# Lagged inputs loaded by lag for a whole slice, squares summed a tile later, remainders issued with the next cast, and other DMA charges in the planner

## The chip, the cores and the metric

The kernel runs on one core of one Trainium2 chip. The metric is device time in microseconds (us): the median of several executions of the whole program, one launch. The profile shows one further execution, which has a time of its own.

## The reference

One inference step of two trunk layers for 256 prompt frames and 32 sample frames (T = 288 columns together), width D = 2048, everything in float32. Layer 0 is attention (eight "fox" heads with forget gates, eight differential heads), layer 1 a diagonal complex state-space layer (S5) with a gated unit behind it. Each layer is adaLN (shift, scale and gate from a conditioning vector) around an RMS norm, and a residual. Cut to what the change touches:

```python
def _rmsnorm(x, g):                        # squares summed over the 2048 channels
    y = x32 * lax.rsqrt(jnp.mean(x32 * x32, axis=-1, keepdims=True) + EPS)
...
def _ssm_layer(x, c, l, isd, s_re, s_im, p):
    h, gate = _adaln(x, c, ...)
    u, z = jnp.split(h @ p['w_in_ssm'][isd], 2, axis=-1)
    y, state = _s5_sequence(u32.reshape(B, T, N_GROUPS, GROUP_CH), ...)
    y = y.reshape(B, T, D_SSM) + p['ssm_d'][isd] * u32
    g = jax.nn.gelu(y)
    glu = g * jax.nn.sigmoid(g @ p['w_glu'][isd] + p['b_glu'][isd])
    out = (glu * jax.nn.silu(z)) @ p['w_out_ssm'][isd]
    x = x + gate * out
```

`_s5_sequence` runs x[t] = a x[t-1] + B u[t], y[t] = C x[t] for 128 groups of 16 channels with 64 complex states each.

## The kernel before, in words

**Layout.** Activations lie transposed: 16 tiles of 128 channels (partitions) by 288 frames. In layer 1 the frames are reordered in blocks of LC = 8: column s * 36 + j is frame 8 j + s, so that NJ = 36 blocks stand side by side for each position s within a block.

**Main matmuls in two parts.** A weight tile `w` is [128, 4, 512], 1 MB. Each of its four quarters is cast by ScalarE to a rounded `hi` (`act.copy`), and VectorE (DVE) subtracts to get the remainder `lo` (`split_step`, L406). Activations are split likewise (`ah`, `al`). For every 128 by 128 block TensorE issues three matmuls (L473 to L475): hi by ah, hi by al, lo by ah. Eight quarters may be live (NQ), four weight buffers exist (NST), with more in the first stage. With the fourth quarter, `st_done` frees the weight buffer and `pump` issues the next weight load on SP.

**Order.** `run_jobs` (L450) goes through a list of jobs, one for each weight tile, and after every second block it calls `split_step` (casts ahead) and `side.step`, which gives a turn to side tasks: Python generators that emit a few instructions and yield until they are due. When a task is due is decided by a planner (`Plan`, `Engine.cost`): each emitted instruction adds an estimated duration to the planned time of its engine, and a task goes on when the planned time of TensorE has reached the planned end of what it waits for. The planner runs while the program is built, so its figures set only the order of instructions on each engine's queue; each engine then executes its queue in order, and semaphores make it wait where data are not there. A DMA's planned cost is bytes / 360 GB/s on one common DMA clock, with 0.6 us ahead and 2.0 us behind (L122 to L131).

**The S5 layer (from L1433).** Jobs: 16 weight tiles of w_in_ssm give u (`u_evac`), 16 give z (`z1_evac`), then 16 of w_glu and 16 of w_out_ssm. Beside them run these side tasks:
- `state_in` (L1587): for each quarter of U (four tiles) it stores U to DRAM (`ud`), loads it regrouped as `ug` with 8 DMAs of 72 KB in 144-byte pieces (in the profile MX<-ud), multiplies (xin_ps) and fills X.
- `scan` (L1627): 32 steps of small DVE instructions for each quarter.
- `slices` (L1669): for each of 16 slices matmuls y_ps from the scanned states (Xm), then stores to `yd` (8 DMAs for four slices).
- `lags` (L1567) and `inside` (L1704): the part of y from within a block of 8 frames. For each slice, TensorE multiplies blocks `kb` by inputs shifted by 0 to 3 block positions (lags): partition 32 l + c of a load holds channel c at lag l. The four groups g of 32 channels (pairs of the reference's groups) of a slice each have a load of their own, `UL[4 i + g]`, [128, 288]:

```python
sp.dma_start(UL[n], bass.AP(ud.tensor, ud.offset + row * (PAD + T),
                            [[NJ, 4], [PAD + T, 32], [1, T]]))
```

Each step and count pair of the source pattern is an axis, slowest first: 4 lags, 32 channels, 288 columns. Five such buffers lie in a freed weight buffer; three more lie in `W1r` once `state_in` is through with it (L1625). The profile names these loads UL<-ud and W1r<-ud. SP issues the loads in order with all weight loads, and a load into a used buffer waits for the matmuls that read it.
- `gelus`, `gelu` (L1726): read `yd`, add, GELU, and an `act_split` makes the GLU's ah and al. U lies in MX, so the profile calls it MX.

**Squares.** `op_evac` (L1345, end of layer 0) and `fin_evac` (L1779, end of layer 1) evacuate an output tile into the residual; then ScalarE squares it into a scratch tile (`yx` in the profile), and DVE adds the square to `ssq1` at once (for tile 0 a copy; the last tile's square goes to the sum over channels by itself, through `ssl`).

All engine calls go through one wrapper, so every instruction of the profile has line L114; tiles tell them apart.

Of the kernel before, what the change touches and what calls it, by code (L numbers as in the profile page):

```python
# [93 lines left out]
class Engine:  # L94
# [5 lines left out]
    def __getattr__(self, fn):  # L100
# [14 lines left out]
        return call  # L115

    def cost(self, fn, out, ins, outs, k):
        p = self.plan
# [3 lines left out]
        if fn == "dma_start":  # L122
            t = max([p.when(p.written, a) for a in ins] + [p.at[self.name], p.base.get(out.tensor.name, 0.0)])
            p.at[self.name] = t + (0.45 if self.name != "pool" else 1.0)
            size = n * out.shape[0] * 4 / 360e3
            if self.name == "act":
                end = t + 2.6 + 2 * size
            else:
                p.at["dma"] = max(p.at["dma"], t + 0.6) + size
                end = p.at["dma"] + 2.0  # L130
            p.note(p.written, out, end)  # L131
            for a in ins:
                p.note(p.read, a, end)
            p.last = max(p.last, end)
            return
# [118 lines left out]
def build(tc, I, O):  # L254
# [8 lines left out]
    with ExitStack() as ctx:  # L263
# [142 lines left out]
        def split_step(t, force=False):  # L406
# [12 lines left out]
            act.copy(hi, st[:, i, :])  # L419
            TT(lo, st[:, i, :], hi.bitcast(F32), ALU.subtract)  # L420
            qs.append((hi, lo))
            split["live"] += 1
            if i == 3:
                st_done(k)
                pump()
            return True

        def order_of(j):
# [21 lines left out]
        def run_jobs(upto, n_side):  # L450
            while pos["run"] < upto:
# [5 lines left out]
                if j["kind"] == "main":  # L457
# [6 lines left out]
                    for i, (n, q, k, begin, end) in enumerate(order_of(j)):  # L464
                        while len(qs) <= q:
                            if not qs:
                                side.upto(plan.when(plan.written, st_of[t]))
                            split_step(t, True)
                        if first and begin:
                            g["ps"][n] = pm.tile([128, 512], F32, tag="m", name="m")  # L470
# [7 lines left out]
                        if last and end:  # L478
                            plan.last = 0.0
                            g["evac"](n, ps[:, 0:N], c)  # L480
                        if i % 2:
                            split_step(t)
                            side.step(n_side)
# [861 lines left out]
        def op_evac(gi):  # L1345
            def ev(n, ps, c):
# [9 lines left out]
                if c == 3:  # L1356
                    sq = scratch(k % 2)[:, 0:T]
                    act.activation(sq, MX[:, slot(k), :], AF.Square)
                    if k == 0:
                        dve.tensor_copy(ssq1, sq)  # L1360
                    elif k < KT - 1:
                        TT(ssq1, ssq1, sq, ALU.add)
                    else:
                        ssl.append(sq)
                    if n == 3:
                        ready.add(("x1", gi))
            return ev

        ssl = []
        op0 = len(jobs)  # L1370
# [191 lines left out]

        def ul_bufs(t, n):

            ul_free.extend(t[:, k * T:k * T + T] for k in range(n))

        def lags():  # L1567

            zero = SZ[:, 0:6, :].rearrange("p a t -> p (a t)")
            pool.memset(zero, 0.0)  # L1570
            sp.dma_start(ud[:, :, 0:PAD].rearrange("n p t -> p n t"), zero.rearrange("p (n t) -> p n t", n=KT))
            while taken[0] is None:
                yield "w any"
            t = wst.tile([128, 2048], F32, tag="w%d" % taken[0], name="UL")
            ul_bufs(t, 5)
            for n in range(4 * KT):
                while ("ur", n // 16) not in ready or not ul_free:
                    yield "w any"
                UL[n] = ul_free.pop(0)
                row = 128 * (n // 4) + 32 * (n % 4)  # L1580
                sp.dma_start(UL[n], bass.AP(ud.tensor, ud.offset + row * (PAD + T),
                                            [[NJ, 4], [PAD + T, 32], [1, T]]))
                if n % 4 == 3:
                    ready.add(("ul", n // 4))
                yield "next any"

        def state_in():  # L1587
# [36 lines left out]
            yield  # L1624
            ul_bufs(w1r[0][0], 3)  # L1625

# [77 lines left out]
        def inside():  # L1704
# [3 lines left out]
            for i in range(KT):  # L1708
                yield from wait(("ul", i))
                kb = kbs.pop(i)  # L1710
                plan.last = max([plan.when(plan.written, UL[4 * i + g]) for g in range(4)] + [plan.when(plan.written, kb)])
                yield "dve"
                yield from room()
                tps = take([128, T], "t_ps")
                for a in range(2):
                    for g in range(4):
                        mm(tps[32 * g:32 * g + 32, 4 * a * NJ:T], kb[:, g, a], UL[4 * i + g][:, 0:T - 4 * a * NJ],
                           start=a == 0, stop=a == 1)
                ul_free.extend(UL.pop(4 * i + g) for g in range(4))
                kb_load(i + 3)  # L1720
# [58 lines left out]
        def fin_evac(gi):  # L1779
            def ev(n, ps, c):  # L1780
# [3 lines left out]
                for b, (j0, j1) in enumerate(((0, JP), (JP, NJ))):  # L1784
                    dve.scalar_tensor_tensor(xk[:, :, j0:j1], ps.rearrange("p (s j) -> p s j", s=LC)[:, :, j0:j1],
                                             gate[:, 1, k, b:b + 1], xk[:, :, j0:j1], op0=ALU.mult, op1=ALU.add)
                sq = scratch(k % 2)[:, 0:T]
                act.activation(sq, MX[:, k, :], AF.Square)
                if k == 0:
                    dve.tensor_copy(ssq1, sq)  # L1790
                elif k < KT - 1:
                    TT(ssq1, ssq1, sq, ALU.add)
                else:
                    ssl.append(sq)
            return ev
# [192 lines left out]
```

## Time and profile before

| | us |
|---|---|
| three runs | 1415.28, 1416.33, 1420.74 (median 1416.33) |
| the profiled execution | 1416.64 |
| its span | 1414.8 |
| TensorE (PE) busy | 1270.3, 90% of the span |
| VectorE (DVE) busy | 928.9, 66% |
| ScalarE (ACT) busy | 594.3, 42% |

The DMA engines moved 344.91 MB, 244 GB/s on average. PE is matmuls, PEld the weight loads of TensorE beside them, SPq the queue of DMA issues on SyncE. In a row of the stage view stand the stretch, its length, then for PE, PEld, DVE, ACT and POOL the busy time with the number of instructions, then the granted TensorE clock (1.00 is full), the mean busy share of the 16 DMA engines and GB/s. In a row of the group view stand what is written from what, the count, busy time and mean duration (ns), and behind the bar the idle time of the engine ahead of them and whose work ended it. In the view of waits stand who waited for whom, the total, how often and the longest. Shares of DMA can exceed 1 where packets overlap.

### The profile page before, as it was taken

How to read it: one execution, taken by the hardware profiler on the slowest of the kernel's cores; microseconds unless marked ns; L12 is line 12 of the kernel's file. 1: busy time of each engine (PE TensorE's matmuls, PEld its weight loads, DVE VectorE, ACT ScalarE, POOL GpSimd, SP SyncE). 2: the span in 40 equal slices, each digit the busy share in tenths (PEclk: the TensorE clock that was granted, in tenths of full speed). 3: DMA queues.
4: the chain of work that ended last, by engine and by line, in shares of the span. 5: the costliest groups of instructions: out<-in, count | busy, mean ns of one | idle time of the engine just before them, and what ended most of it. 6: DMA issues, size and time to landing. Idle time of an engine off the chain costs nothing.

```text
span 1414.8 us, 28189 instructions
## 1 busy us (share of the span) xinstructions
PE 1270.3 (90%) x11098; PEld 1112.1 (79%) x11098; DVE 928.9 (66%) x2212; ACT 594.3 (42%) x1394; POOL 32.6 (2%) x21
## 2 busy tenths in 40 slices
PE   4999899999998999998996978849979877999996
PEld 2788798887887888886896958838869847989995
DVE  4479988697786777887667618527735835455554
ACT  4434233333454454554535624413444534344341
POOL 0005000000000000000000000000000000000000
PEclk9999999999999999999998999978988978999998
DMA  9988696698889898987755877883587645877641
GB/s 316 339 304 309 211 329 249 227 336 293 313 289 312 287 317 298 337 296 271 272 178 137 287 200 174 226 205 104 181 188 201 197 150 155 293 258 266 230 148 68
DMA packets 251011, 344.91 MB, mean 244 GB/s; under 512 B 51424, under 2 KB 141552, under 8 KB 250880
## 3 DMA queue, kind: packets, MB, share of 16 engines
q1 hardware_dynamic: 238208, 313.47, 68.5%
q10 hardware_dynamic: 12672, 29.65, 5.9%
q8 instruction: 88, 1.44, 0.4%
q14 instruction: 43, 0.35, 0.1%
HBM read 307.13 MB, written 35.95 MB: 242 GB/s over the span
## 4 chain that ended last, share of the span: by engine, by line
issue 46%; PE 24%; DVE 13%; DMA 10%; ACT 4%; SPq 1%; ACTq 0%; POOL 0%; POOLq 0%; DVEq 0%
PE m L114 19%; DMA w<-in_w_in_att 5%; DVE lo L114 4%; PE mod_ps L114 3%; DVE v L114 2%; ACT hi L114 2%; DVE MX L114 2%; DMA w<-in_w_mod 2%; DVE tmpv L114 1%; DMA w<-in_w_out_att 1%; SPq L114 1%; DVE qkv L114 1%; DVE dtmp L114 1%; DMA v_d<-v 1%; DMA c_gT<-in_gT 0%
## 5 line engine op out<-in xcount | busy, mean ns | idle before, releaser
L114 PE MATMUL m<-ah,hi 128*128 128x288 f32 (+1 forms) x2304 | 717.2, 311 | 28.3 <-ACT ah L114 14.6
L114 PE MATMUL m<-ah,lo 128*128 128x288 f32 (+1 forms) x2304 | 691.8, 300 | 6.7 <-DVE lo L114 6.6
L114 PE MATMUL m<-al,hi 128*128 128x288 f32 (+1 forms) x2304 | 692.6, 301 | 0.4 <-DVE al L114 0.4
L114 DVE TENSOR_TENSOR lo<-w,hi 128x512 fp32r<-128x512 f32 x560 | 374.2, 686 | 246.3 <-ACT hi L114 236.0
L114 PEld LDWEIGHTS m<-ah,hi 128*128 128x128 f32 x2304 | 444.3, 193 | 94.9 <-issue 41.8
L114 ACT CAST hi<-w 128x512 fp32r<-128x512 f32 x560 | 326.5, 618 | 362.5 <-PE m L114 204.0
L114 PEld LDWEIGHTS m<-ah,lo 128*128 128x128 f32 x2304 | 444.9, 193 | 9.3 <-DVE lo L114 9.3
L114 PEld LDWEIGHTS m<-al,hi 128*128 128x128 f32 x2304 | 445.2, 193 | 1.6 <-DVE al L114 1.4
L114 PE MATMUL mod_ps<-w,cs 128*32 128x512 f32 x736 | 96.2, 617 | 1.9 <-DMA w<-in_w_mod 1.9
L114 DVE SCALAR_TENSOR_TENSOR qkv<-m,qkv 128x288 f32<-128x288 f32 x168 | 73.0, 452 | 26.4 <-PE m L114 26.1
L114 DVE TENSOR_TENSOR X<-X,t 128x32 f32<-128x32 f32 (+1 forms) x256 | 58.3, 228 | 8.2
L114 PE MATMUL t_ps<-UL,kb 128*32 128x288 f32 (+1 forms) x220 | 31.9, 431 | 26.1 <-DMA UL<-ud 26.1
L114 ACT ACTIVATE yx<-MX 128x288 f32<-128x288 f32 (+1 forms) x40 | 19.7, 492 | 70.0 <-DVE MX L114 70.0
L114 DVE TENSOR_TENSOR v<-pt,raw 128x512 f32<-128x512 f32 (+1 forms) x64 | 46.0, 718 | 2.5 <-DMA v_d<-v 2.2
L114 DVE SCALAR_TENSOR_TENSOR MX<-MX,c_dT,t_ps 128x288 f32<-128x288 f32 x16 | 8.2, 514 | 59.0 <-PE t_ps L114 59.0
L114 DVE TENSOR_TENSOR tmpv<-pt,raw 128x512 f32<-128x512 f32 (+1 forms) x64 | 45.9, 717 | 0.0
L114 PE MATMUL y_ps<-Xm,v 128*128 128x74 f32 x256 | 37.4, 309 | 9.1 <-ACT Xm L114 9.1
L114 PEld LDWEIGHTS y_ps<-Xm,v 128*128 128x128 f32 x256 | 35.9, 223 | 10.8 <-ACT Xm L114 10.3
L114 PEld LDWEIGHTS t_ps<-UL,kb 128*32 128x32 f32 x220 | 9.5, 124 | 43.6 <-DMA UL<-ud 35.2
L114 DVE SCALAR_TENSOR_TENSOR MX<-m,gate,MX 128x256 f32<-128x256 f32 x96 | 30.7, 362 | 18.7 <-PE m L114 18.6
L114 PEld LDWEIGHTS mod_ps<-w,cs 128*32 128x32 f32 x736 | 16.9, 110 | 29.4 <-issue 25.6
L114 DVE TENSOR_TENSOR v<-v,tmpv 128x512 f32<-128x512 f32 (+1 forms) x48 | 34.3, 714 | 1.7
(228 smaller groups left out, 921.1 us busy)
## 6 DMA issues: line engine op xcount, KB each, us to landing
w<-in_w_mod SPq DMA_DIRECT2D x128, 512.0 KB
w<-in_w_in_att SPq DMA_DIRECT2D x40, 1024.0 KB
w<-in_w_in_ssm SPq DMA_DIRECT2D x32, 1024.0 KB
w<-in_w_mod SPq DMA_DIRECT2D x28, 1024.0 KB
w<-in_w_in_att SPq DMA_DIRECT2D x48, 512.0 KB
w<-in_w_out_att SPq DMA_DIRECT2D x16, 1024.0 KB
w<-in_w_glu SPq DMA_DIRECT2D x15, 1024.0 KB
w<-in_w_out_ssm SPq DMA_DIRECT2D x13, 1024.0 KB
```

What stands on the lines that cost most here:

```text
L114: return f(*a, **k)
```

## The change

Five edits:
1. The planner charges a DMA by its pieces (contiguous runs on both sides): 12 ns and 0.142 ns an element for each, over 16 engines; and 0.6 us more ahead of it (SP, POOL and ACT queues).
2. A remainder `lo` is no longer emitted with its cast. It is kept in `rests` and emitted with the next cast, when its quarter is needed, or when the planner takes the cast to be over (`rest_due`). Freeing the weight buffer goes with the fourth remainder.
3. A square joins the sum when the next tile's square comes up (`squares`); tile 0's square is written to `ssq1` directly.
4. Lagged inputs: a buffer now holds a whole slice, [128, 4 x 288], and each of its four loads brings one lag, 32 partitions by four groups by 288. Two such buffers exist from the start, the freed weight buffer and a new tile UL1; those in W1r are gone.
5. `inside` reads `UL[i][:, g]` and gives a buffer back by slice.

```diff
+    def pieces(out, src):
+        total, run = 1, []
+        for d in out.shape:
+            total *= d
+        for a in (out, src):
+            r = 1
+            for st, n in reversed(list(a.ap)[1:]):
+                if st != r and n > 1:
+                    break
+                r *= n
+            run.append(r)
+        r = min(run)
+        return total / r * (12 + 0.142 * r) / 16e3
...
-            size = n * out.shape[0] * 4 / 360e3
+            size = self.pieces(out, ins[0])
             if self.name == "act":
-                end = t + 2.6 + 2 * size
+                end = t + 3.2 + 2 * size
             else:
-                p.at["dma"] = max(p.at["dma"], t + 0.6) + size
+                p.at["dma"] = max(p.at["dma"], t + 1.2) + size
                 end = p.at["dma"] + 2.0
...
             act.copy(hi, st[:, i, :])
-            TT(lo, st[:, i, :], hi.bitcast(F32), ALU.subtract)
             qs.append((hi, lo))
             split["live"] += 1
-            if i == 3:
-                st_done(k)
-                pump()
+            rest_step(0)
+            rests.append((k, i, st, hi, lo))
             return True
+        rests = []
+        def rest_step(left):
+            while len(rests) > left:
+                k, i, st, hi, lo = rests.pop(0)
+                TT(lo, st[:, i, :], hi.bitcast(F32), ALU.subtract)
+                if i == 3:
+                    st_done(k)
+                    pump()
+        def rest_due():
+            if rests and plan.when(plan.written, rests[0][3]) <= max(plan.at["dve"], plan.at["pe"]):
+                rest_step(len(rests) - 1)
...
                             split_step(t, True)
+                        if rests and rests[0][:2] <= (t, q):
+                            rest_step(0)
...
                         if i % 2:
+                            rest_due()
                             split_step(t)
                             side.step(n_side)
...
-                    sq = scratch(k % 2)[:, 0:T]
-                    act.activation(sq, MX[:, slot(k), :], AF.Square)
-                    if k == 0:
-                        dve.tensor_copy(ssq1, sq)
-                    elif k < KT - 1:
-                        TT(ssq1, ssq1, sq, ALU.add)
-                    else:
-                        ssl.append(sq)
+                    squares(k, MX[:, slot(k), :])
...
+        def squares(k, x):
+            for sq in sqs:
+                TT(ssq1, ssq1, sq, ALU.add)
+            sqs.clear()
+            sq = scratch(k % 2)[:, 0:T] if k else ssq1
+            act.activation(sq, x, AF.Square)
+            if k == KT - 1:
+                ssl.append(sq)
+            elif k:
+                sqs.append(sq)
...
-            ul_bufs(t, 5)
-            for n in range(4 * KT):
-                while ("ur", n // 16) not in ready or not ul_free:
+            ul_free.extend((t[:, 0:4 * T], sl.tile([128, 4 * T], F32, name="UL1")))
+            row = PAD + T
+            for n in range(KT):
+                while ("ur", n // 4) not in ready or not ul_free:
                     yield "w any"
-                UL[n] = ul_free.pop(0)
-                row = 128 * (n // 4) + 32 * (n % 4)
-                sp.dma_start(UL[n], bass.AP(ud.tensor, ud.offset + row * (PAD + T),
-                                            [[NJ, 4], [PAD + T, 32], [1, T]]))
-                if n % 4 == 3:
-                    ready.add(("ul", n // 4))
+                UL[n] = ul_free.pop(0).rearrange("p (g t) -> p g t", g=4)
+                for l in range(4):
+                    sp.dma_start(UL[n][32 * l:32 * l + 32], bass.AP(ud.tensor, ud.offset + 128 * n * row + l * NJ,
+                                                                    [[row, 32], [32 * row, 4], [1, T]]))
+                ready.add(("ul", n))
                 yield "next any"
...
-            ul_bufs(w1r[0][0], 3)
...
-                        mm(tps[32 * g:32 * g + 32, 4 * a * NJ:T], kb[:, g, a], UL[4 * i + g][:, 0:T - 4 * a * NJ],
+                        mm(tps[32 * g:32 * g + 32, 4 * a * NJ:T], kb[:, g, a], UL[i][:, g, 0:T - 4 * a * NJ],
...
-                ul_free.extend(UL.pop(4 * i + g) for g in range(4))
+                ul_free.append(UL.pop(i).rearrange("p g t -> p (g t)"))
```

`fin_evac` calls `squares(k, MX[:, k, :])` in the same way.

More of the change, by code (lines that the diff above doesn't have):

```diff
@@ L115, in __getattr__ @@
         return call
+    @staticmethod
+    def pieces(out, src):
[11 more added lines that the diff above has]
+        return total / r * (12 + 0.142 * r) / 16e3
     def cost(self, fn, out, ins, outs, k):
@@ L1367, in op_evac @@
             return ev
-        ssl = []
+        ssl, sqs = [], []
+        def squares(k, x):
[8 more added lines that the diff above has]
+                sqs.append(sq)
         op0 = len(jobs)
@@ L1561, in build @@
         UL, ul_free = {}, []
-        def ul_bufs(t, n):
-            ul_free.extend(t[:, k * T:k * T + T] for k in range(n))
         def lags():
@@ L1710, in inside @@
                 kb = kbs.pop(i)
-                plan.last = max([plan.when(plan.written, UL[4 * i + g]) for g in range(4)] + [plan.when(plan.written, kb)])
+                plan.last = max(plan.when(plan.written, UL[i]), plan.when(plan.written, kb))
                 yield "dve"
@@ L1786, in ev @@
                                              gate[:, 1, k, b:b + 1], xk[:, :, j0:j1], op0=ALU.mult, op1=ALU.add)
[L1787 to L1794, printed above, removed]
+                squares(k, MX[:, k, :])
             return ev
```

## The prediction

> **What bounds the kernel now.** I read the page first, then the chain, then busy time by stage, then the waits of the one stage that stands out.
>
> ```profile
> span 1414.8 us, 28189 instructions
> ...
> PE   4999899999998999998996978849979877999996
> ```
> ```profile
> 777.98 624.03 issue
> ```
> TensorE is busy nearly everywhere except from slice 21 to slice 33. The chain of waits is no help there: behind 778 us it is one piece of 624 us that waits for nothing it can name. So the stages are taken from busy times instead, cut where the work changes (0 to 765 attention, 765 to 1191 the S5 layer with its input projections, then GLU and output projection):
>
> ```profile
> core 0: us, PE busy (x) PEld busy (x) DVE busy (x) ACT busy (x) POOL busy (x), PEclk, DMA share, GB/s
> 0.00:318.00 318.00, 289.41 (x2459) 244.71 (x2460) 240.93 (x583) 120.78 (x243) 22.10 (x7) 0.98 0.84 291
> 318.00:765.00 447.00, 425.57 (x4190) 366.37 (x4188) 333.10 (x704) 213.70 (x553) 8.75 (x12) 0.99 0.82 280
> 765.00:1130.00 365.00, 300.20 (x2495) 276.26 (x2496) 209.91 (x659) 150.50 (x394) 0.85 (x1) 0.88 0.71 195
> 1130.00:1162.00 32.00, 22.91 (x116) 11.53 (x116) 9.93 (x17) 13.45 (x35) 0.00 (x0) 0.73 0.47 150
> 1162.00:1191.00 29.00, 21.52 (x147) 20.61 (x145) 17.83 (x28) 12.00 (x20) 0.00 (x0) 0.85 0.77 210
> 1191.00:1379.00 188.00, 187.81 (x1492) 170.99 (x1492) 100.40 (x186) 77.43 (x141) 0.00 (x0) 0.99 0.66 228
> ```
> Idle TensorE is the first column less the second. From 765 to 1191 it is 64.8 + 9.1 + 7.5 = 81.4 us. The same rows show a granted clock of 0.88, 0.73 and 0.85, so busy time there is worth less: 300.2 x 0.12 + 22.9 x 0.27 + 21.5 x 0.15 = 45.4 us more. Some 127 us of this stage is thus neither work nor full speed; the GLU stage behind it loses 0.2 us to idling. Who ended the idle time:
>
> ```profile
> L114 PE MATMUL m<-ah,hi 128*128 128x290 f32 (+1 forms) x561 | 178.4, 318 | 15.7 <-ACT ah L114 14.6 <-DVE MX L114 1.1
> ...
> L114 PE MATMUL y_ps<-Xm,v 128*128 128x74 f32 x256 | 37.4, 309 | 9.1 <-ACT Xm L114 9.1
> L114 PE MATMUL t_ps<-UL,kb 128*32 128x288 f32 (+1 forms) x220 | 31.9, 431 | 26.1 <-DMA UL<-ud 26.1
> L114 PE MATMUL xin_ps<-MX,SZ 128*64 128x36 f32 x320 | 15.0, 262 | 13.0 <-DMA MX<-ud 13.0
> L114 PE MATMUL t_ps<-W1r,kb 128*32 128x288 f32 (+1 forms) x36 | 8.4, 480 | 4.7 <-DMA W1r<-ud 4.7
> L114 PE MATMUL xin_ps<-MX,W1r 128*64 128x36 f32 x192 | 7.6, 240 | 7.4 <-DMA MX<-ud 4.8 <-DMA UL<-ud 2.7
> ```
> Lagged inputs are UL, and W1r where UL uses that tile. They ended 26.1 + 4.7 + 2.7 = 33.5 us of idle time, the largest share. The loads of the regrouped U (`ug`, which the profile calls MX<-ud) ended 13.0 + 4.8 = 17.8 us.
>
> Long waits also cost clock. Two-microsecond rows around one of them:
>
> ```profile
> 922.00:924.00 2.00, 0.00 (x0) 0.00 (x0) 1.84 (x7) 0.46 (x1) 0.00 (x0) 1.00 1.02 244
> ...
> 926.00:928.00 2.00, 0.00 (x0) 0.00 (x0) 0.00 (x0) 0.00 (x0) 0.00 (x0) 0.50 0.29 14
> ...
> 934.00:936.00 2.00, 2.00 (x40) 1.79 (x39) 1.07 (x4) 1.08 (x3) 0.00 (x0) 1.00 1.05 424
> ```
> After some 4 us without matmuls the clock halves, and it is full again only in the row at 934.
>
> **A: the lagged loads.** Why TensorE waits for them shows where little else moves. First SP's issues, then the busy row of that stretch, then TensorE just before:
>
> ```profile
> 1142.31 6.80 SPq L114 DMA_DIRECT2D UL<-ud  x5
> 1149.22 3.35 SPq L114 DMA_DIRECT2D W1r<-ud  x3
> ```
> ```profile
> 1144.00:1154.00 10.00, 8.56 (x40) 4.62 (x42) 3.95 (x6) 4.75 (x12) 0.00 (x0) 0.50 0.27 97
> ```
> ```profile
> 1136.54 0.67 PE L114 MATMUL t_ps<-UL,kb 128*32 128x288 f32 x2 [0.80 <-DMA UL<-ud]
> 1138.44 0.67 PE L114 MATMUL t_ps<-UL,kb 128*32 128x288 f32 x2 [1.23 <-DMA UL<-ud]
> 1140.63 1.28 PE L114 MATMUL t_ps<-UL,kb 128*32 128x288 f32 x10 [1.51 <-DMA UL<-ud]
> ```
> ```profile
> UL<-ud SPq DMA_DIRECT2D x55, 144.0 KB
> ...
> W1r<-ud SPq DMA_DIRECT2D x9, 144.0 KB
> ```
> With only these loads in flight the DMA share is 0.27 and the rate 97 GB/s, though loads were queued throughout; the row at 934 shows 424 GB/s at a share of 1.05. A load of 147,456 bytes at 97 GB/s takes 1.52 us, and TensorE's pairs of matmuls indeed come about 2 us apart, each behind one load. A share of 0.27 is about 4 engines of 16. The old source pattern starts with an axis of 4 (the four lags), the weights' with 128; I conclude that a load runs on as many engines as its first axis lets it. In the new form each load is one lag of a whole slice, and both patterns start with an axis of 32. Bytes, pieces (128 of 1152 bytes) and the number of loads, 64, stay.
>
> The Trainium skill says this outright: "DMA: Bandwidth & Descriptors", section "Why a DMA increments its semaphore by 16 and not by 1", has the number of engines be the largest number up to 16 that divides the slowest axis of both patterns. That gives 4 before, as the row has it, and 16 after. Counting bytes alone, the new layout would be worth nothing (rival 3); by the spread it carries most of the sum.
>
> On 16 engines a load takes 0.38 us, less than SP needs to issue it:
>
> ```profile
> L114 SPq DMA_DIRECT2D UL<-ud x55: 503/527/3488, 821.2 to 1148.6; - x55
> ```
> so loads would come 0.53 us apart instead of 1.52. Of each wait 0.53/1.52 = 35% remains: 33.5 x 0.65 = 22 us gained. Bounds: nothing, if another wait steps in at once, and all 33.5, since the planner's figure for such a load (0.41 us before, 0.42 now) is at last about what it takes, and because two buffers of a whole slice exist from the start, where there were five quarters and eight only once W1r is read. The buffers' price: SP still waits for slice i's matmuls before loading slice i + 2, and weight loads queue behind it as now; I cost that at nothing since those matmuls come sooner.
>
> **B: clock.** The 22 us are 27% of the stage's 81.4 us idle time. I give them the same share of the 45.4 us: 12 us. Bounds 0 and 18.7 (33.5 of 81.4).
>
> **C: what the planner charges for DMA.** Nothing is added to the chip's work; the order of instructions is worked out with other times. For short pieces the change is large. One `ug` load (512 pieces of 36 elements) went from 73,728 bytes / 360 GB/s = 0.205 us to 512 x (12 + 0.142 x 36) ns / 16 = 0.547 us.
>
> ```profile
> 818.00:820.00 2.00, 2.00 (x18) 2.00 (x17) 1.02 (x2) 0.62 (x1) 0.00 (x0) 1.00 1.34 160
> 820.00:822.00 2.00, 1.90 (x15) 1.66 (x13) 0.69 (x1) 0.82 (x2) 0.00 (x0) 1.00 1.25 126
> ```
> ```profile
> MX<-ud SPq DMA_DIRECT2D x32, 72.0 KB
> ```
> While eight of them move, 160 and 126 GB/s carry 572 KB in 4 us, 0.5 us a load: the new figure fits. The planner will thus place the xin matmuls 8 x 0.342 + 0.6 = 3.3 us later in the instruction stream and run main matmuls first.
>
> ```profile
> PE xin_ps L114 <- DMA MX<-ud: 17.8, 3, 6.8
> ```
> Three such waits make up the 17.8 us, so 10 us could go; I take 5, half, because the data come no sooner and the scan starts behind them. Bounds 0 and 17.8. Weight loads move little: 1 MB in 2 KB pieces from 2.91 to 2.71 us, with 0.6 us more ahead of it. That reorders everything before 765 a little; the idle time there is 28.6 and 21.4 us, so I take 0 with 5 us either way, a tenth of it.
>
> **D: squares.** The DVE copy for tile 0 goes, and each addition is issued a tile later, so DVE doesn't stand behind ScalarE's square. Around the first such pass (700 to 780 us):
>
> ```profile
> DVE ssq L114 <- ACT yx L114: 8.5, 15, 0.6
> ...
> PE m L114 <- DVE MX L114: 3.8, 6, 1.1
> ```
> DVE waits 8.5 us, of which 3.8 us reach TensorE through evacuations. I take half, 2 us; bounds 0 and 3.8. At the end, the last square already goes to the sum by itself, so nothing there.
>
> **E: remainders (lo) with the next cast.** DVE's waits at the head of its queue, and what this costs TensorE:
>
> ```profile
> DVE lo L114 <- ACT hi L114: 242.5, 168, 13.8
> ACT hi L114 <- PE m L114: 211.6, 136, 13.8
> ...
> ACT hi L114 <- DMA w<-in_w_in_att: 49.4, 19, 6.3
> ...
> PE m L114 <- DVE lo L114: 6.6, 7, 2.5
> ```
> DVE's 242.5 us are mostly idle time without a customer. Other DVE work may now pass, but the remainder itself comes later. When a quarter is wanted at once, both are still issued together. I take 0. Bounds: a gain of 6, TensorE's other waits for DVE evacuations; a loss of 6.6, its waits for lo doubled.
>
> **Sum.** 22 + 12 + 5 + 2 = 41 us. The profiled execution took 1416.6 us (its span and 1.8 us around it), 0.3 above the median of 1416.33. 1416.6 - 41 = 1375.6, so 1376.
>
> **Rivals.**
> 1. The freed time turns into another wait. The last quarter of U is stored at 1038 (SP's last ud<-MX issue below), after scans that fill DVE; from there scan, y, gelu follow one another until the GLU's last chunk. If that chain sets the stage's end, earlier savings are lost, and only the idle and slow time of the row from 1130 to 1162 counts, 9.1 + 6.2, with 2 for D: 1399. For it: DVE is only 57% busy there, yet TensorE has only 116 matmuls in the 32 us from 1130. Against it: the chain itself holds lagged and ug waits.
>
> ```profile
> 1038.27 0.60 SPq L114 DMA_DIRECT2D ud<-MX  x1
> ```
> 2. Loads into 32 partitions run at half rate: 0.76 us each, half of A's waits remain, A is 17 and B 9, so 1416.6 - 33 = 1384. No row here shows long pieces going to 32 partitions. The Trainium skill, "SBUF — State Buffer", section "Door 1: The DMA port swizzle (why `[64,N]` ≈ `[32,N]`)", has 32 partitions reach 8 of 16 ports, which speaks for this rival; no run here shows it yet.
> 3. The lag form does not do what it says: still 4 engines. Only C and D remain, 7 us: 1410. The trace names no engines, only shares.
> 4. Slower: later remainders hold back weights. The buffer is handed on only with the fourth remainder, and SP waits for exactly that:
>
> ```profile
> SPq L114 <- DVE lo L114: 149.1, 29, 9.4
> ```
> (318 to 765). A quarter lasts 12 matmuls of 188/1492 = 0.126 us, 1.5 us. If the next load of 40 of the 52 weight tiles of that stage (by the code 36 of w_in_att, 16 of w_out_att) came 1.5 us later and TensorE ran dry each time, 60 us: 1436. It decides from 27 tiles on, where it eats the 41 us. Against it: casts wait 211.6 us for free slots and 49.4 us for weights, so weights mostly lie ready.
>
> **Chances and range.** Forecast 0.61, rivals 0.18, 0.07, 0.06, 0.08. About 0.5% (7 us) is what a measurement of this kernel can tell from no change, so the bounds are 1409.2 and 1423.4. The forecast and rivals 1 and 2 are faster but for small tails; rival 3 lies on the edge, mostly "same": 0.86 faster, 0.06 same, 0.08 slower. For the range, all upper bounds together are 33.5 + 18.7 + 17.8 + 3.8 + 6 = 80 us (1337), which needs every term at its best; I stop at 1345. Upward it takes in rivals 1 and 2 and ends at 1408; rivals 3 and 4 and small tails are left out.
>
> **What would show it.** Right: t_ps waiting under 12 us for UL in all; the share in the stretch with lagged loads alone well above 0.27; granted clock from 765 to 1130 above 0.90; xin's waits for MX<-ud nearer 10 than 18; the stage from 765 shorter by about 38. Wrong: a share still near 0.27 (rival 3), loads 0.7 us or more apart (rival 2), Xm or ah waits grown by what UL lost (rival 1), or casts before 765 waiting much longer than 49.4 us for weights (rival 4).

## The result and the profile after

| | us |
|---|---|
| before, four runs beside it | median 1415.8 (1413.05 to 1420.74) |
| after, four runs | median 1350.88 (1347.27 to 1354.22) |
| ratio | 0.9537, 95% interval 0.95 to 0.9574 |
| profiled execution, before and after | 1416.64 and 1351.85 (spans 1414.8 and 1350.0) |

The change saves 65 us. The forecast was 41 us of gain (1376), with a range down to 1345: the side is right, the size a third too small.

The page of the changed kernel, span and TensorE slices:

```profile
span 1350.0 us, 28223 instructions
...
PE   4999899999998999999999997776887999999996
```

TensorE's dip from slice 21 to 33 has become one from 24 to 30. Busy time by stage of the changed kernel, cut at the same microseconds as in the prediction (columns as there):

```profile
0.00:318.00 318.00, 291.31 (x2474) 244.62 (x2475) 244.16 (x592) 121.69 (x246) 22.11 (x7) 0.98 0.85 292
318.00:765.00 447.00, 430.66 (x4300) 372.97 (x4300) 339.84 (x736) 226.96 (x590) 9.69 (x13) 1.00 0.85 288
765.00:1130.00 365.00, 306.93 (x2646) 287.17 (x2645) 222.24 (x664) 160.59 (x410) 0.00 (x0) 0.91 0.78 213
1130.00:1162.00 32.00, 32.00 (x234) 28.99 (x234) 15.25 (x27) 11.71 (x21) 0.00 (x0) 0.97 0.70 243
1162.00:1191.00 29.00, 29.00 (x245) 25.80 (x245) 14.11 (x26) 11.38 (x21) 0.00 (x0) 1.00 0.76 266
```

From 318 to 765 TensorE now does 4300 matmuls where it did 4190, so the stage behind it starts earlier; the two tail rows, with 116 and 147 matmuls before, now hold 234 and 245 and lie in the GLU stage, which runs at full speed. To place the gain, cut by the work: the first matmul of the input projections (290 columns) started at 765.3 and starts at 751.8; the GLU's last chunk started at 1190.4 and starts at 1126.4. The gain is then 13.5 us ahead of the S5 stage, 50.5 in it (425.1 to 374.6) and 0.8 behind it. The prediction had 2 us ahead and 39 in it. In that stage TensorE's idle time fell from 81.1 to 58.5 us and its busy time from 344.4 to 315.7.

Who ended TensorE's idle time from 765 to 1191, the groups that answer to those shown of before:

```profile
L114 PE MATMUL m<-ah,hi 128*128 128x290 f32 (+1 forms) x672 | 209.3, 311 | 2.1 <-ACT ah L114 1.2 <-ACT hi L114 0.9
...
L114 PE MATMUL y_ps<-Xm,v 128*128 128x74 f32 x256 | 35.0, 296 | 11.6 <-ACT Xm L114 11.6
L114 PE MATMUL t_ps<-UL,kb 128*32 128x288 f32 (+1 forms) x256 | 20.4, 451 | 38.8 <-DMA UL<-ud 38.8
L114 PE MATMUL xin_ps<-MX,SZ 128*64 128x36 f32 x320 | 11.4, 228 | 1.0 <-issue 0.7 <-PE m L114 0.3
L114 PE MATMUL xin_ps<-MX,W1r 128*64 128x36 f32 x192 | 9.2, 265 | 3.3 <-DMA UL<-ud 3.3
```

t_ps is what `inside` multiplies, xin_ps what `state_in` multiplies. This is not the picture that was forecast. The waits for lagged loads, which A was to cut from 33.5 us to about 12, are 38.8 + 3.3 = 42.1 us counted as A counted. The 3.3 us, as the 2.7 us before, are better left out: xin_ps reads `ug` and its own weight, no lagged load, and the profile names what landed last. Then t_ps' waits went from 30.8 to 38.8 us. What shrank is the busy time of the same matmuls: 31.9 + 8.4 before, 20.4 now. The waits of xin_ps fell from 20.4 to 4.3 us, and none of them is put down to `ug` any more; of the 14.6 us in which TensorE waited for ScalarE's `ah` 1.2 are left. Now the waits of the whole program that the prediction had for E, then SP's issues of the lagged loads and of U's four stores:

```profile
ACT hi L114 <- PE m L114: 215.7, 135, 9.2
DVE lo L114 <- ACT hi L114: 153.7, 131, 9.8
...
ACT hi L114 <- DMA w<-in_w_in_att: 35.5, 18, 7.2
```
```profile
L114 SPq DMA_DIRECT2D UL<-ud x64: 302/430/1042, 800.3 to 1014.0; - x64
...
L114 SPq DMA_DIRECT2D ud<-MX x4: 370/415/459, 784.7 to 948.1; - x4
```

VectorE stands 89 us less at the head of its queue for a cast, and the last quarter of U is stored at 948.1 instead of 1038.27. The last lagged load is issued at 1014; before, the last three were issued from 1149 on.

### The profile page after: what moved, and what is told of

Read it like the earlier page. It is cut to its first block, busy times and chain, and to the rows that moved or that the text cites. A ratio compares the mean times of both kernels' runs of the same rounds, so it can differ in the third digit from the quotient of the medians.

```text
span 1350.0 us, 28223 instructions
## 1 busy us (share of the span) xinstructions
PE 1235.8 (92%) x11098; PEld 1094.1 (81%) x11098; DVE 920.9 (68%) x2210; ACT 592.6 (44%) x1394; POOL 32.6 (2%) x21
## 4 chain that ended last, share of the span: by engine, by line
issue 44%; PE 33%; DMA 10%; DVE 9%; ACT 3%; SPq 0%; ACTq 0%; POOL 0%; POOLq 0%; DVEq 0%
PE m L114 25%; DMA w<-in_w_in_att 5%; PE mod_ps L114 4%; DMA v_d<-v 2%; DVE lo L114 2%; DMA w_d<-W 2%; DVE v L114 1%; DMA w<-in_w_mod 1%; DVE MX L114 1%; ACT hi L114 1%; DVE qkv L114 1%; DVE tmpv L114 1%; PE w_ps L114 1%; DVE dtmp L114 1%; DMA c_gT<-in_gT 1%
## 5 line engine op out<-in xcount | busy, mean ns | idle before, releaser
L114 ACT CAST hi<-w 128x512 fp32r<-128x512 f32 x552 | 322.2, 618 | 340.0 <-PE m L114 204.6
L114 DVE TENSOR_TENSOR lo<-w,hi 128x512 fp32r<-128x512 f32 x552 | 367.4, 685 | 149.0 <-ACT hi L114 142.4
L114 DVE SCALAR_TENSOR_TENSOR qkv<-m,qkv 128x288 f32<-128x288 f32 x168 | 73.3, 450 | 27.6 <-PE m L114 27.3
L114 PE MATMUL t_ps<-UL,kb 128*32 128x288 f32 (+1 forms) x256 | 20.4, 451 | 38.8 <-DMA UL<-ud 38.8
L114 ACT ACTIVATE yx<-MX 128x288 f32<-128x288 f32 (+1 forms) x38 | 18.9, 496 | 52.1 <-DVE MX L114 51.7
```

The source lines that it names most:

```text
L114: return f(*a, **k)
```

## The experiments

Four theories went in. S: the gain is the spread of a lagged load over 16 engines. P: it is the planner's other order (edit 1). R: it is the remainders (edit 2). Q: it is the squares (edit 3). Edits are numbered as in the section on the change; 4 and 5 go together as "the lag form". Each ratio is against the kernel before on the same chip, and a gain in us is 1416 times what the ratio lacks to 1; it differs from the difference of the medians by up to 2 us. "Store" is SP's issue of U's last quarter, "stage" runs from the first matmul of the input projections to 224 us before the end (where the GLU's last chunk starts: 224.4 us before the end in the kernel before, 223.6 in after). "Ahead of xin" is the order on TensorE's queue, counted in the timelines: how many of the 512 blocks of the input projections (32 weight tiles of 16 blocks) stand ahead of the first xin_ps group of U's last quarter.

| kernel | ratio, 95% | store | start of stage | stage | t_ps busy + waiting | ahead of xin |
|---|---|---|---|---|---|---|
| before | 1 | 1038.3 | 765.3 | 425.5 | 40.3 + 30.8 | 394 |
| squares alone | 0.9968 (0.9944 to 0.9992) | 1032.3 | 765.3 | 419.4 | 40.3 + 24.1 | 394 |
| lag form alone | 0.9801 (0.9775 to 0.9827) | 1029.2 | 767.4 | 399.7 | 19.2 + 27.6 | 390 |
| remainders alone | 0.9804 (0.9773 to 0.9836) | 974.8 | 757.2 | 400.0 | 32.4 + 35.8 | 320 |
| charges alone | 0.9697 (0.9663 to 0.9732) | 966.3 | 764.8 | 389.0 | 38.0 + 38.4 | 328 |
| all but the lag form | 0.9755 (0.9716 to 0.9794) | 988.4 | 756.1 | 401.6 | 39.3 + 44.9 | 396 |
| all but the remainders | 0.9631 (0.9593 to 0.9669) | 968.9 | 764.6 | 370.5 | 20.9 + 24.3 | 332 |
| all but the charges | 0.9532 (0.9498 to 0.9565) | 965.1 | 756.9 | 375.1 | 18.7 + 42.0 | 304 |
| after | 0.9537 (0.95 to 0.9574) | 948.1 | 751.8 | 374.2 | 20.4 + 38.8 | 328 |

### The spread alone, every instruction in its place

This kernel is after in the order of all its instructions; only the source pattern and the target of the lagged loads go back to the old form.

```diff
-                for l in range(4):
-                    sp.dma_start(UL[n][32 * l:32 * l + 32], bass.AP(ud.tensor, ud.offset + 128 * n * row + l * NJ,
-                                                                    [[row, 32], [32 * row, 4], [1, T]]))
+                for g in range(4):
+                    sp.dma_start(UL[n][:, g, :], bass.AP(ud.tensor, ud.offset + (128 * n + 32 * g) * row,
+                                                         [[NJ, 4], [row, 32], [1, T]]))
```

> The changed kernel with every instruction in its place, but each of a slice's four lagged loads brings one group with all four lags (source pattern starts with the axis of 4) into the same buffer, as before the change, instead of one lag of all groups. Theory S (the gain is that a load runs on 16 engines instead of 4): stretches with these loads alone show a DMA share near 0.27 and about 97 GB/s again, a slice's four loads take 6 us, and the time rises by 25 to 45 us, to 1376 to 1396. Theory P (the gain is the order that the planner makes from its new charges, and the form of the loads matters little): under 8 us more, 1351 to 1358.

It took 1395.53 us against 1421.13, ratio 0.9826 (0.9788 to 0.9863), in theory S's range. From there to after the spread is worth 0.0289, about 41 us. That is what is left of it with the new form's price in it: the old form's loads end in 128 partitions, the new form's in 32. TensorE's group in this kernel:

```profile
L114 PE MATMUL t_ps<-UL,kb 128*32 128x288 f32 (+1 forms) x256 | 47.8, 438 | 54.5 <-DMA UL<-ud 53.8 <-issue 0.7
```

Against after the row has 15.7 us more waiting and 27.4 us more busy time, together 43.1, and the spans differ by 43.8. So nearly all of the difference is in this one row, and most of it under "busy". The timelines show what that means; this is the kernel with the old pattern, and behind it after:

```profile
1048.40 1.17 PE L114 MATMUL t_ps<-UL,kb 128*32 128x288 f32 x2 [1.43 <-DMA UL<-ud]
1049.78 1.17 PE L114 MATMUL t_ps<-UL,kb 128*32 128x288 f32 x2 [0.21 <-DMA UL<-ud]
1051.28 1.65 PE L114 MATMUL t_ps<-UL,kb 128*32 128x288 f32 x10 [0.34 <-DMA UL<-ud]
```
```profile
915.31 1.54 PE L114 MATMUL t_ps<-UL,kb 128*32 128x288 f32 x16
```

Behind a load that trickles in, two matmuls count as 1.17 us of work; where the data lie ready, sixteen take 1.54, at a granted clock not much higher (0.50 there, 0.60 here). One matmul lasts as long in both kernels, 438 and 451 ns in the mean. What differs is how many run at once: 256 times 451 ns are 115 us, and in after they fill 20.4 us of TensorE. Where each group's data come alone, its matmuls run alone and fill time that sixteen could have shared. A busy row can hide a wait.

### Each edit alone, and each left out

The edits are those of the diff above, one at a time on the kernel before, or one of them taken back from after. For the charges, for instance:

```diff
-            size = n * out.shape[0] * 4 / 360e3
+            size = self.pieces(out, ins[0])
...
-                p.at["dma"] = max(p.at["dma"], t + 0.6) + size
+                p.at["dma"] = max(p.at["dma"], t + 1.2) + size
```

The lag form alone (edits 4 and 5 on the kernel before):

> The kernel before with the lagged loads by lag and two buffers of a slice alone; charges, remainders and squares as before. Theory S: 1370 to 1385, most of the gain of 65 us. Theory P: 1405 or more, because matmuls are still placed by the old charges and wait where loads queue behind others.

1393.25 us, 28 us gained, between the ranges of the two theories. t_ps lost 21.1 us of busy time and only 3.2 of waiting.

The charges alone (edit 1):

> The kernel before with the planner's new DMA charges alone. Theory S: 1405 to 1416, as the loads still use 4 engines. Theory P: 1365 to 1380.

1378.32 us, 43 us gained, the most of any edit alone and in theory P's range; the forecast had 5. TensorE's xin groups in this kernel:

```profile
L114 PE MATMUL xin_ps<-MX,SZ 128*64 128x36 f32 x320 | 13.1, 244 | 1.6 <-DMA MX<-ud 1.0 <-issue 0.6
...
L114 PE MATMUL xin_ps<-MX,W1r 128*64 128x36 f32 x192 | 6.8, 227 | 1.3 <-DMA UL<-ud 1.3
```

The waits for `ug` fell from 17.8 us to 1.0, those of xin_ps in all from 20.4 to 2.9. These are C's waits, at its upper bound and not at the half that was taken; but C had the xin matmuls placed later and the data "come no sooner". The first quarter's do stand a little later, behind 114 blocks instead of 108. The last quarter's stand 66 blocks sooner, and U's last quarter is stored at 966.25 instead of 1038.27.

The remainders alone (edit 2), against all of after without them:

> The kernel before with the remainders issued with the next cast alone. The stage ahead of 765 us got 11 us shorter in the changed kernel and hardly at all with the charges alone. Theory R (the remainders do it: VectorE lets evacuations pass, so tiles of layer 0 come free sooner): 1400 to 1412 beside a kernel before of 1416. Theory Q (the squares do it): no change, within 7 us. Rival 4 of the prediction (weights held back): slower by 10 us or more.

> The changed kernel with each remainder issued right behind its cast, as before. Theory R: 8 to 12 us above the changed kernel. Theory Q: within 4 us of it; if the remainders cost time in the S5 stage (the kernel with everything but the lag form was slower there than with the charges alone), up to 10 us below it.

1388.02 us alone: 28 us gained where E had 0, and more than theory R's range. Left out of after, they cost 13 (1362.51). The waits of the kernel with the remainders alone:

```profile
DVE lo L114 <- ACT hi L114: 183.0, 142, 9.8
```
```profile
974.82 0.49 SPq L114 DMA_DIRECT2D ud<-MX  x1
```

VectorE's wait at its head fell by 59.5 us, U's last quarter is stored 63 us sooner, and the input projections start at 757.2 instead of 765.3. TensorE's own waits for lo fell too, from 6.6 us to 0.4. That the work queued behind VectorE's wait had a customer after all is one reading. The other is order: the edit also changes the planner's times, and TensorE meets the last quarter's xin after 320 blocks instead of 394. This run changes both and cannot tell them apart. In after the remainders' part lies ahead of the stage: it starts at 764.6 without the remainders and at 751.8 with them, while the stage itself takes 370.5 without and 374.2 with them.

The squares alone (edit 3):

> The kernel before with the squares joining their sum a tile later alone. Theory Q: the wait of 7.2 us of TensorE for ah near 773 us goes, with the shorter waits for VectorE around it, and the time falls by 6 to 12 us. Theory R: within 3 us. Forecast of the prediction: 2 us less.

1410.87 us, 4.5 us gained (interval 1 to 8), where D had 2. That is less than theory Q's 6 to 12, and the wait of 7.2 us for ah near 773 us is still 6.1.

Everything but the lag form (the kernel before's `lags` and `inside`, all else as after):

> The changed kernel with the lagged loads and their buffers as before the change. Theory S: 1385 to 1405. Theory P: 1352 to 1365. Between the two the parts need each other.

1385.06 us, at the lower edge of theory S's range. The lag form is worth 31 us on top of the rest. This kernel is no faster than the charges alone (the intervals touch, its median is the higher one): with the old loads, which hold t_ps for 84 us here, remainders and squares save nothing on top of the charges. The order shows one reason: the last quarter's xin, behind 328 blocks with the charges alone, is back behind 396.

Everything but the charges:

> Kernel after with the planner's old charges of a transfer (0.6 us and bytes over 360 GB/s on the queue); lag form, remainders and squares as in after. Theory P (order: the charges are what moves the last scan and the y groups forward, worth 43 us alone): 1380 to 1390, ratio 0.972 to 0.982, the store of the last quarter of U later than 1000 us, xin's waits for MX<-ud back above 10 us. Theory R (remainders give the same forward move, and the two overlap: 28 and 43 alone): 1355 to 1368, ratio 0.956 to 0.965, the store at 975 to 990 us, as with the remainders alone.

1352.95 us, the same as after within the intervals. Neither theory's numbers hold. P loses: the edit that gains 43 us alone gains nothing in company. R was nearer, but stopped short of this. The table says why as far as it can: with the old loads the stage is 425 us, with either order edit 389 to 400 and with both 402; with the lag form it is 400, with either order edit 370 to 375, and with both 374. Charges and remainders each bring U's last store from 1038 to about 970 and the last quarter's xin 66 to 74 blocks forward, and with the lag form the second edit finds that done. The order leaves main matmuls for the end of the stage: before, with the squares or the lag form alone and with all but the lag form the last y_ps group stands behind all 512 blocks, in the other kernels with an order edit behind 434 to 468. Whether the place on the queue, the store's time or VectorE's shorter wait is the cause, no run isolates: they moved together in all of them.

### What a lagged load costs by itself

After, with idle loads behind the last output into a buffer that nobody reads any more: four of 590 KB into 128 partitions, four of 590 KB into 32 partitions by lag, sixteen of 147 KB in the old form.

```diff
+        row = PAD + T
+        for j in range(4):
+            sp.dma_start(SZ[:, 4 * j:4 * j + 4, :], bass.AP(ud.tensor, ud.offset + 512 * j * row,
+                                                            [[row, 128], [128 * row, 4], [1, T]]))
+        for l in range(4):
+            sp.dma_start(SZ[32 * l:32 * l + 32, :, :], bass.AP(ud.tensor, ud.offset + l * NJ,
+                                                               [[row, 32], [32 * row, 16], [1, T]]))
+        for n in range(16):
+            sp.dma_start(SZ[:, n, :], bass.AP(ud.tensor, ud.offset + 32 * n * row,
+                                              [[NJ, 4], [row, 32], [1, T]]))
```

> The changed kernel with idle loads behind its last output, in three groups that wait for one another and write a tile nobody reads: 4 loads of 590 KB into 128 partitions, 4 of 590 KB into 32 partitions each (one lag of four slices), 16 of 147 KB in the old form (first axis 4). All have pieces of 1152 bytes. By the spread over engines: about 390 GB/s, then 390, then 97 at a share of 0.25. If loads into 32 partitions reach only half of what 128 do (rival 2): the second group at about 200 GB/s.

One run, 1397.39 us with the added loads. Its rows of two microseconds with nothing else in flight (last two columns: mean share of the 16 DMA engines, GB/s), one of the first group, two of the second, two of the third:

```profile
1350.00:1352.00 2.00, 0.00 (x0) 0.00 (x0) 0.00 (x0) 0.00 (x0) 0.00 (x0) 0.50 1.08 389
...
1358.00:1360.00 2.00, 0.00 (x0) 0.00 (x0) 0.00 (x0) 0.00 (x0) 0.00 (x0) 0.50 1.09 210
...
1362.00:1364.00 2.00, 0.00 (x0) 0.00 (x0) 0.00 (x0) 0.00 (x0) 0.00 (x0) 0.50 1.09 212
...
1372.00:1374.00 2.00, 0.00 (x0) 0.00 (x0) 0.00 (x0) 0.00 (x0) 0.00 (x0) 0.50 0.27 97
...
1384.00:1386.00 2.00, 0.00 (x0) 0.00 (x0) 0.00 (x0) 0.00 (x0) 0.00 (x0) 0.50 0.27 97
```

The old form runs at 97 GB/s with a share of 0.27, as in the trace of before. The new form keeps all engines busy, share 1.09, but moves 210 GB/s; into 128 partitions it is 389. At that rate a lagged load of 147,456 bytes takes 0.70 us, not the 0.38 of step A. The share alone does not tell the last two apart.

The old form's share agrees with what the Trainium skill states in "DMA: Bandwidth & Descriptors", section "Why a DMA increments its semaphore by 16 and not by 1": a slowest axis of 4 gives 4 engines. That 32 adjacent partitions run at about half rate agrees with "SBUF — State Buffer", section "Door 1: The DMA port swizzle (why `[64,N]` ≈ `[32,N]`)", by which they reach 8 of 16 ports: 210 of 389 GB/s is 0.54.

### All engines and all partitions

If width is what is left, the lags can be interleaved: partition 4c + l holds channel c at lag l, so that a load of one group has a first axis of 32 and ends in 128 partitions. The small weight is loaded in the same order. TensorE, VectorE and ScalarE keep after's order.

```diff
-                for l in range(4):
-                    sp.dma_start(UL[n][32 * l:32 * l + 32], bass.AP(ud.tensor, ud.offset + 128 * n * row + l * NJ,
-                                                                    [[row, 32], [32 * row, 4], [1, T]]))
+                for g in range(4):
+                    sp.dma_start(UL[n][:, g, :], bass.AP(ud.tensor, ud.offset + (128 * n + 32 * g) * row,
+                                                         [[row, 32], [NJ, 4], [1, T]]))
...
-                sp.dma_start(kbs[i].rearrange("p g a e -> p (g a e)"), kb_d[i])
+                src = kb_d[i]
+                sp.dma_start(kbs[i].rearrange("p g a e -> p (g a e)"),
+                             bass.AP(src.tensor, src.offset, [[256, 32], [32 * 256, 4], [1, 256]]))
```

> Kernel after with the four lags interleaved over the partitions (partition 4c+l holds channel c of a group at lag l, instead of 32l+c): each load still has 147 KB in 128 pieces, its outermost axis still has 32 steps, but it now ends in all 128 partitions instead of 32. The small weight of the lags is loaded in the same permuted order. Order on TensorE, VectorE and ScalarE is that of after. Theory W (the waits that are left at t_ps, 38.8 us in after, are the width of the transfer: 207 GB/s into 32 partitions against 389 into 128): 64 loads become 0.71 - 0.38 = 0.33 us shorter each, 21 us of transfer time; t_ps waits fall to 15 to 28 us, the DMA share of the stage falls from 0.79 towards 0.74, the ratio is 0.940 to 0.948. Theory O (those waits are the place of the loads in SP's row behind weights and stores, and SP's own waits, not their width): t_ps waits stay at 34 to 40 us, the ratio at 0.951 to 0.957.

1333.29 us, ratio 0.94 (0.9372 to 0.9429): theory W, whose waits were to be 15 to 28 us. Its group:

```profile
L114 PE MATMUL t_ps<-UL,kb 128*32 128x288 f32 (+1 forms) x256 | 26.1, 412 | 14.2 <-DMA UL<-ud 14.2
```

Waiting fell by 24.6 us, busy rose by 5.7 (a load now brings one group, so a group's matmuls can start ahead of the rest and trickle a little again): 18.9 us, and the span fell by 19.0. The earlier start of single groups can't be what saves this: behind the last load of a slice ten matmuls are left here that take 0.92 us at best, where all sixteen in after take 0.94 at best.

Two attempts at the rest. First, the planner also reckons that a load waits for the last reader of its buffer:

```diff
-            t = max([p.when(p.written, a) for a in ins] + [p.at[self.name], p.base.get(out.tensor.name, 0.0)])
+            t = max([p.when(p.written, a) for a in ins] + [p.at[self.name], p.base.get(out.tensor.name, 0.0), p.when(p.read, out)])
```

> Interleaved, and the planner also reckons that a load cannot start before the last reader of its buffer (after's planner starts it when its source and its queue are free). Theory O (the t_ps matmuls are placed too early, since the planner leaves out that a load waits for its buffer): t_ps waits fall by at least 10 us below those of interleaved alone, the ratio by 0.007 or more. Theory W: t_ps waits as in interleaved to within 5 us, ratio the same to within 0.004.

1330.17 us, ratio 0.9386 (0.9358 to 0.9414), t_ps waiting 17.8 us: no difference that can be told. Theory O falls. Then, on top of it, eleven buffers of one group instead of two of a slice:

```diff
-            ul_free.extend((t[:, 0:4 * T], sl.tile([128, 4 * T], F32, name="UL1")))
+            t1 = sl.tile([128, 4 * T], F32, name="UL1")
+            ul_free.extend([t[:, k * T:k * T + T] for k in range(7)] + [t1[:, k * T:k * T + T] for k in range(4)])
...
+                UL[n] = []
+                for g in range(4):
+                    while not ul_free:
+                        yield "w any"
+                    UL[n].append(ul_free.pop(0))
...
-                ul_free.append(UL.pop(i).rearrange("p g t -> p (g t)"))
+                ul_free.extend(UL.pop(i))
```

> Interleaved_reuse with the lagged inputs in eleven buffers of one group each (seven in the weight buffer, four in a tile of their own) in place of two of a slice, each handed back after its slice's matmuls: a load of the slice after next can be under way before the slice ahead is done with. Order on TensorE shifts a little where the loads come earlier. Theory B (the t_ps waits that are left, 17.8 us, are loads held on SP until the last reader of one of only two slice buffers): t_ps waits fall to 8 us or less, the ratio from 0.9386 to 0.928 to 0.935. Theory N (the loads are not held by their buffers but stand on SP behind weights and U's stores): t_ps waits stay at 13 to 20 us, the ratio at 0.935 to 0.942.

1328.12 us, ratio 0.938 (0.9348 to 0.9412), t_ps waiting 20.6 us: theory B falls, and N's 13 to 20 us are nearly met. More buffers do not shorten these waits. The longest wait that is left in after shows where the loads stand. First SP's queue, then TensorE:

```profile
908.28 15.01 SPq L114 DMA_DIRECT2D yd<-Yg  x8
923.38 1.49 SPq L114 DMA_DIRECT2D w<-in_w_in_ssm  x1
924.97 0.45 SPq L114 DMA_DIRECT2D kb<-kb_d  x1
925.48 3.24 SPq L114 DMA_DIRECT2D UL<-ud  x4
928.82 0.68 SPq L114 DMA_DIRECT2D kb<-kb_d  x1
929.54 5.75 SPq L114 DMA_DIRECT2D UL<-ud  x4
```
```profile
936.99 1.67 PE L114 MATMUL t_ps<-UL,kb 128*32 128x288 f32 x16 [10.97 <-DMA UL<-ud]
```

The lagged loads stand behind eight stores of y, with which SP is done after 15 us, and are issued up to 935. The stores themselves are not that slow: a merged row holds its gaps too. The profile's view of waits has SP standing still between them for 10.2 of the 15.01 us (2.6, 1.1 and 6.5), and for 3.5 us more between the last four loads, each time until a transfer issued before had landed. From 905 to 915 the DMA share was 1.06 and 1.08. So in this stretch it is the transfers ahead that hold the loads back, as far as one wait can show; no run moved them. The three interleaved kernels beat both original ones; among themselves they can't be told apart.

## Why the prediction came out as it did

**A, lagged loads (22 us; measured 28 alone, 31 on top of the rest, the spread alone 41).** That the old form runs on 4 engines and the new on 16 agrees with the shares of 0.27 and 1.09, and the spread is the largest lasting part. Its working was wrong in two places, so that 22 came near 28 is in part luck. A load takes 0.70 us and not 0.38, which is rival 2's mechanism; its time of 1384 was missed because the other steps gave more. And the gain was worked out from idle time alone, of which 35% was to remain. t_ps' waits went from 30.8 us to 27.6 in the old order and from 54.5 to 38.8 in after's order, so 90% and 71% remained; after's order asks for the loads sooner. t_ps' busy time halved from 40.3 to 20.4. The rows "TensorE's pairs of matmuls indeed come about 2 us apart" were quoted, but not counted as a cost. The sign "under 12 us for UL" did not come; the share did rise, to 1.09 with only such loads in flight, and the granted clock from 765 to 1130 to 0.91.

**B, clock (12 us).** Of the right kind, its size not isolated: the stage's mean clock rose from 0.87 to 0.91, and its busy time fell by 29 us, of which 19.9 are t_ps'; the other 9 are what a faster clock can account for (the 304 us beside t_ps would be some 13 less at 0.91 than at 0.87).

**C, charges (5 us; measured 43 alone, nothing on top of the rest).** All but 1.0 of the 17.8 us of waits for `ug` went, and the order also put the last quarter's xin 66 blocks and U's last store 72 us ahead, where C had the xin matmuls later and the data no sooner.

**E, remainders (0; measured 28 alone, 13 on top of the rest).** This step failed outright. "DVE's 242.5 us are mostly idle time without a customer" was argued from TensorE's 6.6 us of waits for lo, which count one customer only: the scans and evacuations that stand behind lo on VectorE, and the stores that need them, never show as waits for lo. Nor did E ask what the edit does to the order, as C did for the charges, and the last quarter's xin moved 74 blocks forward. The bound of 6 us was therefore no bound. TensorE's waits for lo fell by 6.2 us; how the rest of the 28 divides between order and VectorE's 59.5 us stays open. Rival 4 did not come: from 318 to 765 ScalarE's casts waited 30.2 us for w_in_att and 13.6 for w_out_att, 43.8 in all, where it had been 40.5 and 4.8.

**D, squares (2 us).** 4.5 us alone; its interval of 1 to 8 takes in the 2.

**Rival 1** named the right chain, U's late store after scans that fill VectorE. The prediction took it for something that caps the gain; it moves with two of the edits. The lag form alone leaves the store at 1029 and reaches 1393, near rival 1's 1399; the other edits carried the time from there to 1351.

**The sum.** 41 was forecast and 65 measured. Terms measured alone are 28 + 43 + 28 + 4.5 = 103.5, so adding them would have been wrong too: charges and remainders overlap nearly in full inside the stage. 1350.88 lies in the range because its lower end nearly held all terms at their bounds. That is luck: C and E each gave more alone than their bounds of 17.8 and 6, and only their overlap keeps the time above 1345. Of idle time A and C forecast 27 us less in the stage, and 22.6 went, but t_ps' part of it grew, and what went were mostly waits for `ah` (13.4) and of xin_ps (16.1).

## What to carry to other kernels

When an engine waits at the head of its queue, ask who needs what stands behind the waiting instruction, and not only who needs its result. An edit that changes when an instruction is emitted here changes the planner's order as well: count in the timeline what stands ahead of a group before and after. Count matmuls that follow loads one by one as waiting, whatever the busy column says: compare with the same matmuls where the data lie ready. And read a transfer's rate beside its share: a first axis that spreads over all engines and a target that spreads over all partitions are two conditions, each worth a factor here (97, 210 and 389 GB/s).

## What the runs showed of the hardware

With pieces of 1152 bytes and nothing else in flight, four engines, counted by the share, moved 97 GB/s, sixteen into 32 partitions 210 and sixteen into 128 partitions 389; the share read 0.27, 1.09 and 1.08. SP's issue of a lagged load took 0.43 us in the median in after and 0.60 in the interleaved kernel, so it is not the 0.53 us of the prediction whatever the form. SP was done with eight stores of y after 15.01 us in after, and after 8.53 in the kernel with eleven buffers:

```profile
905.86 8.53 SPq L114 DMA_DIRECT2D yd<-Yg  x8
```

The difference is waiting: SP stood still for 10.2 us between the stores in the first kernel and 3.8 in the second, which leaves 4.8 and 4.7 us for the stores. Each wait ended with a transfer that had been issued before; why SP needs it to land was not tried.
